# A third place in PSUM for the products of w_up, reordered joints between chunks, and a reordered end in a one-core trunk layer

## The chip, the cores and the metric

One kernel computes one layer of a diffusion backbone on one core of one Trainium2 chip. The metric is the device time in microseconds of one execution; lower is better. The engines named below are TensorE (PE in the rows; PEld is its weight load), VectorE (DVE), ScalarE (ACT), GpSimd (POOL) and SyncE (SP, which issues nearly all DMAs). SBUF is the on-chip memory that all engines work on, PSUM the accumulators that TensorE writes.

## What is computed

The layer has a mixer part (attention and a state-space scan, until about 800 us) and a ConvFFN. The change touches the second alone:

```python
h2 = rmsnorm(x, norm_ffn_g) * (1 + sc2) + sh2
u  = dwconv_centred(h2 @ w_up, ffn_conv_w, ffn_conv_b)      # width 3 along the tokens
x  = x + g2 * ((silu(u[..., :D_FF]) * u[..., D_FF:]) @ w_down)
y  = rmsnorm(x, final_norm_g)
```

There are 640 tokens (128 of a prompt and 512 of a sample, with their own modulation), a width of 1024 and D_FF = 2816. Data and results are float32. Tokens lie along the free axis, features along the 128 partitions.

## The kernel before

Each float32 operand of a matmul is split into a rounded part `hi` and a rest `lo` (line 112 computes the rest, line 115 the rounding), and a product is the sum of hi·hi, hi·lo and lo·hi (`mm3`, line 139).

The 2816 features are 22 tiles of 128. A tile i has two products of w_up: (i,0), the gate, and (i,1), the value. Each takes 8 blocks of the width, three matmuls each, on 384 and 256 columns: 48 matmuls. It goes into one of two PSUM buffers called `big` (two banks each, so that 640 columns fit). The buffers go round, so that product n + 2 has to wait until the convolution of product n has read its buffer. The convolution (`conv`, lines 463 to 468) is one pass on ScalarE (scale and bias of the middle tap) and four on VectorE, which add the two neighbour taps for each of the two token groups. The fourth, line 468 on 511 columns, frees the buffer. Behind the value comes the join: silu on ScalarE (L1258) and the product of gate and value on VectorE (L1434). Tile (1,0) is an exception: its product was made before, in an SBUF tile, and its convolution (`early`) reads SBUF alone.

Beside this runs work for later: the weights of the next products are loaded and split (rounding on ScalarE, rest on GpSimd); after every odd tile the two joined tiles are cut into blocks (`blocks`, L1266 to L1281) and split; and after some tiles `ada_next` computes a column of the modulation on VectorE, two passes over 1024 columns each (L260). The table `ADA` says how many such columns follow tile i.

The tiles come in chunks that begin at 0, 8 and 16 (`CHUNKS`). At the end of a chunk, its tiles times w_down are added to x. Here a fast product for 2×2 blocks is used: seven products instead of eight, with sums and differences of blocks of weights (`Pair.add`, L1330) and of the results (L1361 and the lines below). A pair stands for two output tiles; four pairs make a chunk's 1024 outputs. Each of the seven products takes an operand (`put`), which is a rounding on ScalarE and a rest on GpSimd or, where `ON_DVE` says so, on VectorE. A joint is the place where a chunk ends: the two products of the next tile (nxt,0) and (nxt,1) stand there, then the pairs. `LEAD` = 5 operands are made ahead of the first product of a pair.

At the end, the outputs 4 to 7 of the last chunk are made by plain products (`plain`, L1523): first on 384 columns (c0), then on 256 (c1), 16 matmuls each. Behind each stands `residual` (VectorE, L1098) and a square for the final norm (`finished`, ScalarE, L1535). `sumsq` (L166) adds the squares over the partitions with matmuls of one column; `rstd_cols` (L171, L172) takes the root and the reciprocal, `diag` (L177) puts it on a diagonal, a matmul with ones (L1597, L185) spreads it over the partitions, and `scaled_out` (L1583) scales and issues a DMA to `out_y` for each output and column part: 16 in all, on SP.

The order on the compute engines is partly found by a scheduler when the program is built; within `tc.manual_schedule` (the joints with the pairs, and the end) the order is that of the code, and `issue_after` holds an instruction behind another.

## Time and profile before

| | us |
|---|---|
| three runs: median (lowest, highest) | 1265.67 (1265.47, 1268.54) |
| the profiled execution | 1265.61 |
| its span, first to last instruction | 1263.8 |
| TensorE busy | 1197.4 (95 %) |
| VectorE busy | 861.4 (68 %) |
| ScalarE busy | 589.2 (47 %) |
| GpSimd busy | 498.3 (39 %) |

The span runs from the first instruction to the last; what lies between it and the time of the execution is start and end of the program. Busy shares are means over the whole program. In the rows a name such as `big<-pg,whi` says what is written from what; x4 counts instructions drawn together; the square brackets give the idle time of the engine just before and the engine, buffer and line that ended it. A clock of 1.00 in a window is the full 2.4 GHz of TensorE, 0.50 is 1.2 GHz.

### The profile page before, as it was taken

The numbers are of one execution on the slowest core, as the hardware profiler recorded it, in microseconds if no ns is written. First come the engines' busy times: TensorE is split into PE (matmuls) and PEld (weight loads), VectorE is DVE, ScalarE is ACT, GpSimd is POOL, SyncE is SP. The second block draws the span as 40 slices with busy tenths as digits, with TensorE's granted clock in tenths as the row PEclk, the third lists the DMA queues.
The fourth block names the chain that finished last, engine by engine and source line by source line (L and its number), as shares of the span: only waits on it lengthen the run. The fifth ranks groups of instructions, "written<-read, shape, count | busy, mean of one in ns | idle before, by whom it ended". The sixth has DMA issues, their size and how long they took to land. (4 is left out here: it accounts for less than half of the span.)

```text
span 1263.8 us, 21105 instructions
## 1 busy us (share of the span) xinstructions
PE 1197.4 (95%) x8273; PEld 1144.8 (91%) x8273; DVE 861.4 (68%) x1516; ACT 589.2 (47%) x1086; POOL 498.3 (39%) x304
## 2 busy tenths in 40 slices
PE   7798999999999899999979898999999999999996
PEld 5698999989999898888968897999999999999996
DVE  4766656575547566776869898877785456875755
ACT  5455455544647645544762233544333433434432
POOL 3433121221213342554657484543255333454422
PEclk9999999999999899999979899999999999999998
DMA  8333221222128653312465664233246221362222
GB/s 328 126 104 111 71 71 62 78 72 99 38 92 285 215 193 115 99 66 100 139 228 184 210 223 172 83 117 125 68 143 229 79 70 48 109 201 75 86 74 84
DMA packets 59107, 160.31 MB, mean 127 GB/s; under 512 B 6784, under 2 KB 12736, under 8 KB 59008
## 3 DMA queue, kind: packets, MB, share of 16 engines
q1 hardware_dynamic: 56960, 156.33, 36.5%
q10 hardware_dynamic: 2048, 2.63, 0.7%
q8 instruction: 65, 1.06, 0.4%
q14 instruction: 34, 0.28, 0.1%
HBM read 130.82 MB, written 25.59 MB: 124 GB/s over the span
## 5 line engine op out<-in xcount | busy, mean ns | idle before, releaser
L139 PE MATMUL big<-pg,whi 128*128 128x384 f32 (+2 forms) x3264 | 636.1, 314 | 16.1 <-DVE pg L468 7.9
L139 PEld LDWEIGHTS big<-pg,whi 128*128 128x128 f32 x3264 | 497.8, 189 | 31.3 <-issue 12.4
L112 POOL TENSOR_TENSOR wlo<-raw,whi 128x512 fp32r<-128x512 f32 (+3 forms) x161 | 305.8, 1908 | 539.9 <-ACT whi L115 531.1
L139 PE MATMUL big<-pg,wlo 128*128 128x384 f32 (+2 forms) x1632 | 384.0, 311 | 4.6 <-POOL wlo L112 4.6
L139 PEld LDWEIGHTS big<-pg,wlo 128*128 128x128 f32 x1632 | 255.6, 190 | 5.9 <-POOL wlo L112 5.4
L115 ACT CAST whi<-raw 128x512 fp32r<-128x512 f32 (+3 forms) x186 | 138.1, 758 | 154.3 <-issue 74.1
L139 PE MATMUL sm<-pg,whi 128*128 128x320 f32 (+2 forms) x584 | 135.5, 317 | 7.5 <-ACT pg L115 4.1
L139 PEld LDWEIGHTS sm<-pg,whi 128*128 128x128 f32 x584 | 100.4, 191 | 11.0 <-ACT pg L115 4.4
L139 PE MATMUL sm<-pg,wlo 128*128 128x320 f32 (+2 forms) x292 | 91.8, 314 | 0.4 <-POOL wlo L112 0.4
L465 DVE SCALAR_TENSOR_TENSOR st<-big,vec,st 128x127 f32<-128x127 f32 x68 | 37.0, 544 | 67.6 <-ACT st L463 67.6
L112 POOL TENSOR_TENSOR wlo<-sum,whi 128x512 fp32r<-128x512 f32 (+1 forms) x40 | 50.1, 1275 | 61.3 <-ACT whi L115 61.3
L115 ACT CAST pg<-pg 128x640 fp32r<-128x640 f32 (+1 forms) x60 | 40.4, 706 | 69.5 <-DVE pg L1088 35.1
L112 DVE TENSOR_TENSOR pg<-pg,pg 128x640 fp32r<-128x640 f32 (+1 forms) x57 | 52.7, 949 | 11.4 <-ACT pg L115 11.4
L260 DVE SCALAR_TENSOR_TENSOR araw<-araw,crow 128x1024 f32<-128x1024 f32 x32 | 58.4, 1826 | 0.6
L139 PEld LDWEIGHTS sm<-pg,wlo 128*128 128x128 f32 x292 | 55.9, 191 | 0.7 <-POOL wlo L112 0.7
L112 DVE TENSOR_TENSOR ptl<-sm,pth 128x512 fp32r<-128x512 f32 (+1 forms) x48 | 29.6, 620 | 35.0 <-ACT pth L610 35.0
L594 ACT ACTIVATE p<-sm,st 128x320 f32<-128x320 f32 x64 | 33.1, 523 | 37.7 <-DVE st L592 37.7
L591 DVE TENSOR_REDUCE st<-sm 128x1 f32<-128x320 f32 (+1 forms) x72 | 31.5, 462 | 26.6 <-PE sm L587 26.6
L260 DVE SCALAR_TENSOR_TENSOR junk<-araw,crow 128x1024 f32<-128x1024 f32 x32 | 47.4, 1482 | 0.0
L610 ACT CAST pth<-sm 128x512 fp32r<-128x512 f32 (+1 forms) x48 | 25.5, 533 | 43.6 <-PE sm L607 43.5
L465 DVE SCALAR_TENSOR_TENSOR pg<-big,vec,pg 128x127 f32<-128x127 f32 (+1 forms) x42 | 22.8, 543 | 30.5 <-ACT pg L463 30.5
L115 ACT CAST whi<-sum 128x512 fp32r<-128x512 f32 (+1 forms) x40 | 22.6, 596 | 40.5 <-DVE sum L1330 30.1
(323 smaller groups left out, 1947.3 us busy)
## 6 DMA issues: line engine op xcount, KB each, us to landing
raw<-w_up SPq DMA_DIRECT2D x44, 512.0 KB, 3.5
araw<-w_adar SPq DMA_DIRECT2D x32, 512.0 KB, 4.0
araw<-w_ada SPq DMA_DIRECT2D x16, 512.0 KB, 7.3
raw<-w_down SPq DMA_DIRECT2D x16, 512.0 KB, 3.5
raw<-w_xbc SPq DMA_DIRECT2D x12, 512.0 KB, 3.4
scr_xc<-pg SPq DMA_DIRECT2D x16, 320.0 KB, 3.5
pg<-scr_xc SPq DMA_DIRECT2D x16, 320.0 KB, 4.2
raw<-w_gm SPq DMA_DIRECT2D x8, 512.0 KB, 3.3
```

The source lines that it names most:

```text
L112: return eng.tensor_tensor(out, x, f(hi), ALU.subtract)
L115: ACT.copy(hi, src)
L139: PE.matmul(o, w, r[:, s], start=first and i == 0, stop=last and i == 2, skip_group_check=on)
L260: DVE.scalar_tensor_tensor(out, raw, 1.0, crow[r], ALU.mult, ALU.mult, accum_out=mod[:, j, r : r + 1])
L465: DVE.scalar_tensor_tensor(dst[:, lo_ + 1 : hi_], p[:, lo_ : hi_ - 1], vec[:, w : w + 1], dst[:, lo_ + 1 : hi_], ALU.mult, ALU.add)
L591: DVE.reduce_max(st[:, i : i + 1], sv, AX.X)
L594: ACT.activation(p[:, i * w : (i + 1) * w], sv, AF.Exp, bias=st[:, 2:3], scale=SCALE, accum_out=st[:, 4 + i : 5 + i])
L610: return ph, pl, ACT.copy(ph[:, :n], pt[:, :n]), sub(DVE, pl[:, :n], pt[:, :n], ph[:, :n])
```

## The change

Six things are changed.

1. *A third place in PSUM.* The value product (i,1) of an even tile (2, 4, ... 20) goes into two small PSUM buffers of one bank each (384 and 256 columns), which come from the pool the pairs use; all others stay in `big`. Its convolution, `conv_parts`, has two passes on ScalarE (L1265 of the changed kernel) and six on VectorE (L1273), since the columns lie in two buffers. Before, of the products (2,0), (2,1), (3,0), (3,1), (4,0) each waits for the one two places ahead of it; now (3,0) waits for the buffer of (1,1), (3,1) for that of (2,0), (4,0) for that of (3,0), and (5,0) for that of (3,1).
2. *The start.* The early convolution (1,0) is issued behind the last step of (0,1)'s convolution.
3. *ADA* is (0, 0, 2, 1, 2, 1, 2) instead of (0, 1, 1, 1, 1, 2, 2).
4. *The joint.* The loads for the pairs and the sums of the first pair come one product earlier (with tile (nxt−1,0)); its first five operands come later, all behind silu(nxt,0); and the seventh operand of a chunk's first pair has its rest made on GpSimd. The sums of the next pair stand one behind each product instead of two behind the third.
5. *The last pairs:* sums and operands of their first come after the first plain products.
6. *The end.* The squares of c0 are added on VectorE before `sumsq`, which has three matmuls instead of nine and stands behind product 5 instead of product 4; the spreading matmul comes behind product 6 instead of 5; the outputs of c1 go in four DMAs of two tiles each, issued by SP and ScalarE in turn, to a new output array that the host joins to the rest.

```diff
-LEAD, ON_DVE = 5, (4, 6)
+LEAD, ON_DVE = 5, ((4,), (4, 6))
-ADA = (0, 1, 1, 1, 1, 2, 2)
+ADA = (0, 0, 2, 1, 2, 1, 2)
...
         def product(self):
+            if self.j and self.i % 2 == 0 and self.i:
+                outs = [(small()[:, 0 : c.stop - c.start], c) for c in PARTS]
+                for k in range(8):
+                    (hi, lo), s = self.w[k // 4], slice(k % 4 * 128, k % 4 * 128 + 128)
+                    mm3(outs, hi[:, s], lo[:, s], h2[k], k == 0, k == 7)
+                return [o for o, _ in outs]
             ps = big()
...
+    def conv_parts(dst, ps, w, b):
+        for p, c in zip(ps, PARTS):
+            ACT.activation(dst[:, c], p, AF.Identity, bias=vec[:, b : b + 1], scale=vec[:, w + 1 : w + 2])
+        for d, t in ((-1, 0), (1, 2)):
+            for lo_, hi_ in ((0, NP), (NP, T)):
+                for p, c in zip(ps, PARTS):
+                    r0, r1 = max(c.start, lo_ + (d > 0)), min(c.stop, hi_ - (d < 0))
+                    if r0 < r1:
+                        o = dst[:, r0 - d : r1 - d]
+                        ev = DVE.scalar_tensor_tensor(
+                            o, p[:, r0 - c.start : r1 - c.start], vec[:, w + t : w + t + 1], o, ALU.mult, ALU.add
+                        )
+        return ev
...
-            self.w.append(operand(x, self.n * 128, DVE if n in ON_DVE else POOL))
+            self.w.append(operand(x, self.n * 128, DVE if n in ON_DVE[self.m > 0] else POOL))
...
-                for n in ((), (), (1, 2), (3,), (), (4,), ())[s]:
+                for n in ((), (), (1,), (2,), (3,), (4,), ())[s]:
                     nxt.add(n)
...
-        us[i, j] = up_conv(i, j, p)
+        if (i, j) == (1, 0):
+            with tc.issue_after(after_[0].ins):
+                us[i, j] = up_conv(i, j, p)
+        else:
+            us[i, j] = up_conv(i, j, p)
...
+                if (i, j) == (nxt - 1, 0):
+                    made[i, 1] = Up(i, 1)
+                    made[i, 1].fetch()
+                    ahead = [Up(nxt, 0).load(), Up(nxt, 1).load()]
+                    new = [Pair(c, m) for m in range(0, 8, 2)]
+                    new[0].load()
                 if (i, j) == (nxt - 1, 1):
-                    ahead = [Up(nxt, 0), Up(nxt, 1)]
                     for v in ahead:
                         v.fetch()
-                    new = [Pair(c, m) for m in range(0, 8, 2)]
-                    new[0].load()
+                up_tile(u, early if (i, j) == (1, 0) else None)
+                if (i, j) == (nxt - 1, 0):
                     ready(new[0])
-                    for n in range(LEAD - 1):
-                        new[0].put(n)
-                up_tile(u, early if (i, j) == (1, 0) else None)
...
             silu(us[nxt, 0])
-            new[0].put(LEAD - 1)
+            for n in range(LEAD):
+                new[0].put(n)
...
+        for o, x in ((sq4, sq5), (sq6, sq7), (sq4, acc[:, c0]), (sq4, sq6)):
+            DVE.tensor_tensor(o, o, x, ALU.add)
...
             plain(m, ps, c1, ks)
-            if m == 4:
-                ss = sumsq([acc, sq4, sq6], c0)
...
             if m == 5:
+                ss = sumsq([sum0], c0)
+            if m == 6:
                 rp = small()[:, 0:HALF]
                 PE.matmul(rp, ones, dg, start=True, stop=True)
...
             residual(x2[m], ps, 40 + m, x2[m], c1)
             finished(m, c1, c1 if m < 7 else None)
+            if m == 5:
+                dg = ws.tile([128, HALF], F32, tag="dg", name=nm("dg"), bufs=1)
+                diag(dg, rstd_cols(ss, D, 3))
+            if m == 6:
+                scaled_out(rp, range(4))
...
+        for m in range(8):
+            if m == 1:
+                ACT.copy(rps, rp)
+            o, x = outs[m // 4][:, m % 4], x2[m][:, c1]
+            if m in BY_POOL:
+                POOL.tensor_tensor(o, x, rps, ALU.mult)
+            else:
+                DVE.scalar_tensor_tensor(o, x, vec[:, V_GFIN + m : V_GFIN + m + 1], rp, ALU.mult, ALU.mult)
+            if m % 2:
+                q = nc.sync if m % 4 == 1 else nc.scalar
+                q.dma_start(a["out_z"][:, m - 1 : m + 1], outs[m // 4][:, m % 4 - 1 : m % 4 + 1])
```

Three places show how the instructions move. First VectorE at the start of the ConvFFN, before: `big_8473` holds (0,0) and `big_8536` (0,1); `pg_8325` is the product of (1,0) in SBUF, which the early convolution reads.

```order
L465 SCALAR_TENSOR_TENSOR pg_8522<-big_8473,vec,pg_8522 128x127
L468 SCALAR_TENSOR_TENSOR pg_8522<-big_8473,vec,pg_8522 128x127
L465 SCALAR_TENSOR_TENSOR pg_8522<-big_8473,vec,pg_8522 128x511
L465 SCALAR_TENSOR_TENSOR pg_8593<-pg_8325,vec,pg_8593 128x127
L468 SCALAR_TENSOR_TENSOR pg_8522<-big_8473,vec,pg_8522 128x511
L468 SCALAR_TENSOR_TENSOR pg_8593<-pg_8325,vec,pg_8593 128x127
L465 SCALAR_TENSOR_TENSOR pg_8593<-pg_8325,vec,pg_8593 128x511
L465 SCALAR_TENSOR_TENSOR st_8585<-big_8536,vec,st_8585 128x127
L468 SCALAR_TENSOR_TENSOR pg_8593<-pg_8325,vec,pg_8593 128x511
L468 SCALAR_TENSOR_TENSOR st_8585<-big_8536,vec,st_8585 128x127
```

After, the same place:

```order
L465 SCALAR_TENSOR_TENSOR pg_8522<-big_8473,vec,pg_8522 128x127
L468 SCALAR_TENSOR_TENSOR pg_8522<-big_8473,vec,pg_8522 128x127
L465 SCALAR_TENSOR_TENSOR pg_8522<-big_8473,vec,pg_8522 128x511
L468 SCALAR_TENSOR_TENSOR pg_8522<-big_8473,vec,pg_8522 128x511
L465 SCALAR_TENSOR_TENSOR st_8585<-big_8536,vec,st_8585 128x127
L468 SCALAR_TENSOR_TENSOR st_8585<-big_8536,vec,st_8585 128x127
L465 SCALAR_TENSOR_TENSOR st_8585<-big_8536,vec,st_8585 128x511
L468 SCALAR_TENSOR_TENSOR st_8585<-big_8536,vec,st_8585 128x511
L465 SCALAR_TENSOR_TENSOR pg_8593<-pg_8325,vec,pg_8593 128x127
L1468 TENSOR_TENSOR pg_8522<-pg_8522,st_8585 128x640
L468 SCALAR_TENSOR_TENSOR pg_8593<-pg_8325,vec,pg_8593 128x127
L465 SCALAR_TENSOR_TENSOR pg_8593<-pg_8325,vec,pg_8593 128x511
```

The four steps on (0,0) now stand together, the four on (0,1) follow, and the early convolution's are mixed with the join of tile 0 and its first block difference.

Second, ScalarE at the first joint, before: from the pass over (8,0) (`big1499`) to the copy of the first pair's first result. `whi1501` is the fifth operand; the four ahead of it stand further up, around (7,1).

```order
L463 ACTIVATE pg1500_9662<-big1499_9613,vec_69 128x640
L115 CAST pg1495_9602<-pg1490_9590 128x640
L115 CAST hf1497_9607<-pg1468_9479 128x320
L1258 ACTIVATE pg1500_9662<-pg1500_9662 128x640
L115 CAST whi1501_9669<-raw1478_9509 128x512
L463 ACTIVATE st1508_9730<-big1507_9681,vec_69 128x640
L115 CAST whi1501_9669<-sum1483_9519 128x512
L1358 COPY o31512_9754<-big1509_9739 128x320
```

After; `big1498` is (8,0), `sm1510` and `sm1511` are (8,1):

```order
L463 ACTIVATE pg1499_9662<-big1498_9613,vec_69 128x640
L115 CAST hf1496_9607<-pg1478_9507 128x320
L1288 ACTIVATE pg1499_9662<-pg1499_9662 128x640
L115 CAST whi1500_9669<-raw1475_9454 128x512
L115 CAST whi1500_9669<-sum1480_9515 128x512
L115 CAST whi1502_9675<-sum1481_9517 128x512
L115 CAST whi1502_9675<-sum1479_9513 128x512
L115 CAST whi1504_9681<-raw1475_9454 128x512
L1265 ACTIVATE st1512_9743<-sm1510_9693,vec_69 128x384
L1265 ACTIVATE st1512_9743<-sm1511_9694,vec_69 128x256
L115 CAST whi1504_9681<-sum1482_9519 128x512
L1388 COPY o31516_9770<-big1513_9755 128x320
```

The first five operands of the pair (`whi1500`, `whi1502` and half of `whi1504`) now stand between the silu of (8,0) and the passes over (8,1), where one stood before.

Third, VectorE at the end, before: from the sums of squares to the first scaled output. `sm_13109` and `sm_13110` are the plain products 4 and 5 of c1.

```order
L1577 TENSOR_TENSOR pg_13082<-pg_13082,pg_13089 128x384
L1578 TENSOR_TENSOR pg_13096<-pg_13096,pg_13103 128x384
L172 RECIPROCAL rst_13141<-rst_13141 128x3
L177 TENSOR_SCALAR dg_13144<-cons,rst_13141 128x128 x3
L1098 SCALAR_TENSOR_TENSOR pg_12849<-sm_13109,mod,pg_12849 128x256
L1098 SCALAR_TENSOR_TENSOR pg_12851<-sm_13110,mod,pg_12851 128x256
L1583 SCALAR_TENSOR_TENSOR pg_12841<-pg_12841,vec,sm_13170 128x384
```

After; `sm_13151` and `sm_13152` are products 4 and 5, `sm_13153` is product 6:

```order
L1613 TENSOR_TENSOR pg_13122<-pg_13122,pg_13129 128x384
L1613 TENSOR_TENSOR pg_13136<-pg_13136,pg_13143 128x384
L1613 TENSOR_TENSOR pg_13122<-pg_13122,pg_12748 128x384
L1613 TENSOR_TENSOR pg_13122<-pg_13122,pg_13136 128x384
L1099 SCALAR_TENSOR_TENSOR pg_12889<-sm_13151,mod,pg_12889 128x256
L1099 SCALAR_TENSOR_TENSOR pg_12891<-sm_13152,mod,pg_12891 128x256
L172 RECIPROCAL rst_13204<-rst_13204 128x3
L177 TENSOR_SCALAR dg_13203<-cons,rst_13204 128x128 x3
L1099 SCALAR_TENSOR_TENSOR pg_12893<-sm_13153,mod,pg_12893 128x256
L1620 SCALAR_TENSOR_TENSOR pg_12881<-pg_12881,vec,sm_13228 128x384
```

The reciprocal and the diagonal moved behind the residuals of products 4 and 5, two additions came in, and the first scaled output stands behind product 6's residual.

## Rows read from the trace of the kernel before

**Rows 1.** waits of TensorE from 800 us on; total us, times, longest us

```profile
PE big L139 <- DVE pg L468: 7.9, 4, 3.6
...
PE sm L139 <- DVE o L1361: 1.9, 3, 0.9
```

**Rows 2.** timeline of TensorE; start, us, engine, line, operation, [idle before and releaser]

```profile
806.06 0.82 PE L139 MATMUL big<-pg,whi 128*128 128x384 f32 x4 [1.63 <-DVE pg L468]
...
887.38 0.82 PE L139 MATMUL big<-pg,whi 128*128 128x384 f32 x4 [3.64 <-DVE pg L468]
...
923.47 0.56 PE L139 MATMUL sm<-pg,whi 128*128 128x320 f32 x2 [0.88 <-DVE o L1361]
...
1053.87 0.83 PE L139 MATMUL big<-pg,whi 128*128 128x384 f32 x4 [1.67 <-DVE pg L468]
```

**Rows 3.** windows: length, busy us of PE, PEld, DVE, ACT, POOL; clock, DMA, GB/s

```profile
888.00:893.00 5.00, 5.00 (x26) 5.00 (x25) 4.89 (x9) 0.57 (x2) 1.59 (x1) 0.66 0.34 94
...
1243.00:1248.00 5.00, 5.00 (x29) 4.79 (x28) 1.64 (x6) 0.68 (x2) 0.73 (x1) 0.66 0.01 3
```

**Rows 4.** timeline of VectorE, first tiles of the ConvFFN

```profile
802.93 0.35 DVE L468 SCALAR_TENSOR_TENSOR pg<-big,vec,pg 128x127 f32<-128x127 f32 x1
...
803.86 1.40 DVE L465 SCALAR_TENSOR_TENSOR pg<-pg,vec,pg 128x127 f32<-128x127 f32 x1
...
805.18 0.74 DVE L468 SCALAR_TENSOR_TENSOR pg<-big,vec,pg 128x511 f32<-128x511 f32 x1
...
806.46 1.77 DVE L465 SCALAR_TENSOR_TENSOR pg<-pg,vec,pg 128x511 f32<-128x511 f32 x1
...
831.22 0.82 DVE L1434 TENSOR_TENSOR pg<-pg,st 128x640 f32<-128x640 f32 x1
```

**Rows 5.** timeline of VectorE, from the join of tile 6

```profile
891.55 0.83 DVE L1434 TENSOR_TENSOR pg<-pg,st 128x640 f32<-128x640 f32 x1
...
892.29 1.22 DVE L260 SCALAR_TENSOR_TENSOR junk<-araw,crow 128x1024 f32<-128x1024 f32 x1
...
899.88 0.74 DVE L468 SCALAR_TENSOR_TENSOR pg<-big,vec,pg 128x511 f32<-128x511 f32 x1
```

**Rows 6.** timeline of VectorE, splits at the first joint

```profile
916.19 0.69 DVE L112 TENSOR_TENSOR wlo<-raw,whi 128x512 fp32r<-128x512 f32 x1 [1.37 <-ACT whi L115]
...
921.23 1.78 DVE L112 TENSOR_TENSOR wlo<-raw,whi 128x512 fp32r<-128x512 f32 x1
```

**Rows 7.** timeline of TensorE, the end

```profile
1240.79 0.68 PE L166 MATMUL sm<-cons,pg 128*128 128x1 f32 x4
...
1242.08 1.72 PE L166 MATMUL sm<-cons,pg 128*128 128x1 f32 x14 [0.61 <-DVE pg L1578]
...
1250.19 1.60 PE L1523 MATMUL sm<-pg,pg 128*128 128x256 f32 x12
...
1252.23 0.28 PE L1523 MATMUL sm<-pg,wlo 128*128 128x256 f32 x1
...
1255.54 0.67 PE L185 MATMUL sm<-dg,cons 128*128 128x256 f32 x2 [1.16 <-DVE dg L177]
```

**Rows 8.** timeline of ScalarE, the end

```profile
1241.14 1.28 ACT L171 ACT_TABLE_LOAD   x1
```

**Rows 9.** timeline of VectorE, the end

```profile
1256.65 2.44 DVE L1583 SCALAR_TENSOR_TENSOR pg<-pg,vec,sm 128x256 f32<-128x256 f32 x6 [1.26 <-ACT pg L1608]
```

**Rows 10.** timeline of SyncE's DMA queue, the end

```profile
1260.81 0.40 SPq L1613 DMA_DIRECT2D out_y<-pg  x1
```

**Rows 11.** DMA from 1245 to 1264 us: rate by slice; issues, KB, us to landing

```profile
GB/s 0 0 0 0 0 0 0 0 0 16 352 366 366 142 0 246 362 369 265 49 359 378 42 0 0 0 0 11 272 270 274 274 272 272 267 276 22 0 0 17
...
out_y<-pg SPq DMA_DIRECT2D x8, 128.0 KB, 1.8
```

**Rows 12.** DMA issues of the whole program

```profile
scr_xc<-pg SPq DMA_DIRECT2D x16, 320.0 KB, 3.5
...
out_ssd<-k SPq DMA_DIRECT2D x2, 256.0 KB, 2.0
```

More of the change, by code (lines that the diff above doesn't have):

```diff
@@ L1233, in load @@
             nc.sync.dma_start(self.raw, a["w_up"][2 * self.i + self.j])
+            return self
         def put(self, n):
@@ L1239, in fetch @@
             if not self.w:
-                self.load()
+                if not self.raw:
+                    self.load()
                 self.put(0)
@@ L1250, in product @@
             return mid(ps)
+    def conv_parts(dst, ps, w, b):
[7 more added lines that the diff above has]
+                        o = dst[:, r0 - d : r1 - d]
+                        ev = DVE.scalar_tensor_tensor(
+                            o, p[:, r0 - c.start : r1 - c.start], vec[:, w + t : w + t + 1], o, ALU.mult, ALU.add
+                        )
+        return ev
+    after_ = []
     def up_conv(i, j, p):
         u = stage() if j else page()
-        conv(u, p, V_FW + 3 * (2 * i + j), V_FB + 2 * i + j)
+        ev = (conv_parts if isinstance(p, list) else conv)(u, p, V_FW + 3 * (2 * i + j), V_FB + 2 * i + j)
+        if (i, j) == (0, 1):
+            after_.append(ev)
         return u
@@ L1491, in trunk_kernel @@
                 new[0].load()
-                ready(new[0])
-                for n in range(LEAD):
-                    new[0].put(n)
     def cut(i, c):
@@ L1554, in trunk_kernel @@
         wlast = []
+        ready(new[0])
+        for n in range(LEAD):
+            new[0].put(n)
         new[0].load_x()
@@ L1589, in trunk_kernel @@
             plain(m, ps, c1, ks)
-            if m == 4:
-                ss = sumsq([acc, sq4, sq6], c0)
-                st = rstd_cols(ss, D, 3)
-                dg = ws.tile([128, HALF], F32, tag="dg", name=nm("dg"), bufs=1)
-                diag(dg, st)
             if m == 5:
+                ss = sumsq([sum0], c0)
+            if m == 6:
                 rp = small()[:, 0:HALF]
                 PE.matmul(rp, ones, dg, start=True, stop=True)
-            if m > 5:
-                scaled_out(rp, c0, range(3 * m - 18, 3 * m - 15))
             residual(x2[m], ps, 40 + m, x2[m], c1)
             finished(m, c1, c1 if m < 7 else None)
+            if m == 5:
[3 more added lines that the diff above has]
+                scaled_out(rp, range(4))
         ss = sumsq([acc, sqs[7]], c1)
-        scaled_out(rp, c0, range(6, 8))
+        scaled_out(rp, range(4, 7))
         for m in BY_POOL:
             ACT.activation(x2[m][:, c1], x2[m][:, c1], AF.Copy, scale=vec[:, V_GFIN + m : V_GFIN + m + 1])
-        rp = rstd_rows(ss, D, c1)
-        rps = page()[:, 0:w1]
-        ACT.copy(rps, rp)
-        for m in BY_POOL:
-            POOL.tensor_tensor(x2[m][:, c1], x2[m][:, c1], rps, ALU.mult)
-        scaled_out(rp, c1, [m for m in range(8) if m not in BY_POOL])
-        for m in BY_POOL:
-            nc.sync.dma_start(a["out_y"][m][:, c1], x2[m][:, c1])
+        dg = ws.tile([128, HALF], F32, tag="dg", name=nm("dg"), bufs=1)[:, 0:w1]
+        diag(dg, rstd_cols(ss, D, w1 // 128))
+        scaled_out(rp, range(7, 8))
+        rp = small()[:, 0:w1]
+        PE.matmul(rp, ones, dg, start=True, stop=True)
+        rps = page()[:, 0:w1]
+        outs = [rawtile().rearrange("p (m c) -> p m c", c=w1) for _ in range(2)]
+        for m in range(8):
[9 more added lines that the diff above has]
+                q.dma_start(a["out_z"][:, m - 1 : m + 1], outs[m // 4][:, m % 4 - 1 : m % 4 + 1])
 def _consts():
@@ L1719 @@
 _OUTS = {
-    "out_y": (8, 128, T),
+    "out_y": (8, 128, HALF),
+    "out_z": (128, 8, T - HALF),
     "out_ckv": (2, 128, NP),
```

18 lines of the change are left out of this document (9 added, 9 removed).

## The prediction

> **What bounds the kernel now.** I read the waits of TensorE first, then its timeline at each wait, then what the releasing engine did just before. From 800 us on, where the diff first touches an instruction, TensorE has few stalls, and two releasers hold most of them: the last convolution step (VectorE, L468) frees a `big` buffer too late four times, and L1361 frees a pair's PSUM buffer late three times [rows 1]. So the stage is bound by TensorE and each late release adds to the time directly; VectorE decides when the release comes. The time of a product of w_up follows from two rows: between 806.06 and 887.38 − 3.64 = 883.74 stand 11 products without a gap, 7.06 us each [rows 2]. The longest wait has a second price: after it the granted clock of 888 to 893 us is 0.66, so part of those 5 us ran at 1.2 instead of 2.4 GHz, which loses (1 − 0.66) × 5 = 1.7 us of work; the same 1.7 us is lost after 1243 us [rows 3]. At the end, TensorE's last product is over at 1252.51 (call this X), and 10 us of a serial chain and output transfers follow.
>
> All terms are made against the profiled execution: 1265.61 us, of which 1263.8 are span and 1.8 lie around it. That is the median of the runs (1265.67) within 0.06 us, so I carry gains straight over.
>
> **Start of the ConvFFN.** In before, an SBUF-only convolution step of tile (1,0), 1.40 us (803.86), stands ahead of the L468 that frees the buffer of (0,0); product (1,1) starts at 806.06 after 1.63 us of waiting [rows 2, 4]. After, the order has the four steps of (0,0) together. The release comes at 803.86 + 0.08 + 0.74 = 804.7 instead of 805.18 + 0.74 = 805.9; with 0.05 of spare handover I take **gain 1.3**.
>
> The postponed steps come back later. Steps of (1,0) now stand behind (0,1)'s, which begin behind ScalarE's pass at about 805.6 (by hand) and end at 805.6 + 0.35 + 0.35 + 0.74 + 0.74 = 807.8 (sizes in [rows 4]); with their own four (beside GpSimd's splits the short first took 1.40 and a long one 1.77 in before, so 5 to 6 us), the join of tile 0 and one block difference, they end at about 815.5. The silu of (1,0) stands ahead of (1,1)'s first ACT pass on ScalarE, so conv (1,1) ends at about 820. In before join (2) began at 831.22, 4.0 us behind the end of product (2,1) at 806.06 + 3 × 7.06 = 827.24 [rows 2, 4]; that product now ends 1.3 earlier, and join (2) comes at 830.0 if TensorE alone limits it. If VectorE does, it comes some 13 us behind conv (1,1): join (1), three block differences, four splits and two convolutions, while one ADA step with two passes of 1.22 [rows 5] leaves this stretch; that is an estimate, 833.0. From a join with two ADA steps behind it to the end of the next tile's convolution pass 900.62 − 891.55 = 9.07 us [rows 5]: (3,0)'s buffer comes free at 839.1 to 842.1. The change puts the products (i,1) of even i in the small buffers, and so (4,0) waits for (3,0)'s buffer, which it had not to before; it is due at 840.05 (five products of 7.06 after 804.75). The bounds are 0 and 2.1; I take the later half because the silu is certain to be in the way: **loss 1.5**.
>
> **Steady tiles.** The new rotation of `big` asks that the first convolution of an odd i ends within one product (7.06) of its product's end, for (4,0), (6,0), (8,0) and their like; (7,0) and (15,0) wait for nothing new. The parted convolution has six VectorE steps instead of four: two more starts, at 0.35 − 127 × (0.74 − 0.35)/384 = 0.22 us each, so 0.4 us [rows 4]. An even tile's second product ends at E, its join begins at E + 4.0 as join (2) did, with the parts E + 4.4, the next convolution ends 9.07 later, at E + 13.5, and E + 14.1 (two products) is needed: 0.6 us spare. If these lengthen by more than this, each such tile waits (rival 1). (7,0) no longer waits: 3.64 and the 1.7 of the clock behind it: **gain 5.3** (bounds 3.6 and 5.3). (15,0): **gain 1.67** (bounds 0.8, if half comes back as another wait, and 1.67) [rows 2, 3]. (8,0) is due just when conv (7,0) lands, as sums and two ADA steps lie ahead of it: **loss 0.3**, bounds 0 and 1.2. The fourth wait, 7.9 less the three shown = 0.96 [rows 1], is (20,0)'s; a sum of the last pair still stands ahead of the L468 that frees its buffer, so I leave it: 0, bounds 0 and a gain of 0.96.
>
> **The two joints.** Product 3 waited 0.88 us at 923.47 (and as much at the other joint) for L1361, which stood behind the split L112 of 1.78 us on VectorE [rows 2, 6]. That split goes to GpSimd, and L1361's successor stands right behind the join: I expect 0.3 left. Against this, five splits of the pair's first weights now come after silu(nxt,0) instead of before; the first products' weights are ready near the end of product (nxt,1), so 0.1 lost. **Gain 0.5 at each joint, 1.0 in all**; bounds: all 0.88 gained, and a loss of 1.8 at each, if the first product waits for one whole split beside VectorE. The third place's 0.18, the rest of the 1.9 in [rows 1], I take as gained: **0.2**.
>
> On VectorE the same split takes 0.69 us at 916.19 and 1.78 us at 921.23 [rows 6]. The Trainium skill ("SBUF — State Buffer", section "SBUF: two separate sides") says that VectorE and GpSimd share a port pair which is locked exclusively, the loser standing still. It speaks against this part of the change: more splits on GpSimd next to VectorE's joins would hand the 1.1 us difference between the two rows to the join. By it the joint would gain nothing; by the removed 1.78 alone it gains 0.6.
>
> **The end.** Before, 18 narrow sum-of-squares matmuls stand between products 4 and 5, four from 1240.79 and fourteen from 1242.08 behind a wait of 0.61, and product 5 runs in the stretch of clock 0.66 [rows 3, 7]. After, product 5 follows product 4 directly: 1240.9 + 2.15 = 1243.05 (2.15 is 1252.51 − 1250.19 = 2.32 at full clock, less the 0.17 by which neighbours overlap). Then sums of one tile, a third as many: 0.7; product 6 ends at 1245.9. The row sum's matmul must wait for residual and square behind product 5 (estimated 1.05, so 1244.1), the table load of 1.28 [rows 8], which now stands behind these squares, then root, reciprocal and diagonal (estimated 1.5 with handovers): 1246.9. So a new wait of about 0.9; then about 0.35 for that matmul, half of the 0.67 of its like at 1255.54, since the next product runs into it, and product 7: X' = 1246.9 + 0.35 + 2.15 = 1249.4, **gain 3.1** (bounds: 1.4 if the new wait costs the clock 1.7 again; 4.0 without the wait).
>
> From X to the end of the row sum's second matmul nothing changes, 1255.54 + 0.67 − 1252.51 = 3.7 [rows 7]. VectorE then does its six products of 2.44 us without waiting 0.37 for ScalarE's copy [rows 9]; all outputs are computed at X' + 6.2. Before, the eight issues on SP ran until 1260.81 [rows 10], 8.3 us after X, and the last transfer took 1.8 us from its issue [rows 11]. After there are four transfers of 256 KB by two queues, the last at X' + 6.2. The nearest row for 256 KB to HBM is 2.0 us, the next is 3.5 us for 320 KB [rows 12]; I take 2.0. Last landing at X' + 8.2 instead of X + 10.05: **gain 1.65** (bounds 0.2 and 1.8).
>
> The eight transfers of 128 KB moved at 267 to 276 GB/s [rows 11], so the end may be bound by bytes: 1 MB at 270 GB/s is 3.9 us; begun at X' + 4.6 with about 1 us of latency it ends at X' + 9.5. The Trainium skill ("DMA: Bandwidth & Descriptors", section "Issuing engines are not separate DMA queues") says transfers of all issuing engines share the same 16 engines and a second issuer only saves its sequencer's time. By that rule with this rate the end gains 0.55, by the issue row 1.65.
>
> **Sum.** 1.3 − 1.5 + 5.3 + 1.67 − 0.3 + 1.0 + 0.2 + 3.1 + 1.65 = 12.4 us: 1265.6 − 12.4 = **1253.2 us**.
>
> **Rivals.**
> 1. *Slower: the waits move to the odd tiles.* (4,0), (6,0) and (8,0) now need a buffer that the convolution of the odd tile before frees, with an even tile's join and two ADA steps ahead of it on VectorE. If these 9.07 us grow by g, each waits g − 0.6 and pays 1.7 for the clock as (7,0) did, 3 × (g + 1.1); that eats the remaining gains of 12.4 + 1.5 + 0.3 = 14.2 from g = 3.6 on, 12.7 us in place of 9.07. With g = 6, two sums and a few splits at the slow 1.78, it is 21.3: 1265.6 − 14.2 + 21.3 = 1272.7. For it: sums, splits and ADA steps all stand there. Against: one lengthening beside GpSimd is 1.1 us [rows 6], and it takes four of them in each tile. 5 %.
> 2. *Part of the gain is given back.* (4,0) waits 2.1 and pays 1.7 for the clock, (8,0) 1.2, the joints gain nothing, the new wait at the end costs 1.7: 1253.2 + (2.1 − 1.5) + 1.7 + (1.2 − 0.3) + 1.0 + 1.7 = 1259.1. For it: in both places where TensorE's work thinned out, the clock fell [rows 3]. Against: waits of 1.63 and 1.67 show no lost clock. 24 %.
> 3. *The end is bound by bytes:* 1.1 less gain, 1254.3. 15 %.
> 4. *Better:* (4,0) doesn't wait and (20,0) loses its wait: 1253.2 − 1.5 − 0.96 = 1250.7. 12 %.
> The forecast itself (within 1.5 us) has 44 %.
>
> **How the numbers follow.** A change under 0.3 % (3.8 us) can't be told from none here: faster means below 1261.9, slower above 1269.4. Forecast, rivals 3 and 4 and nearly all of rival 2 are faster: 0.89. The outer part of rival 2, where several of its costs come out above the bounds named, and half of rival 1 (g of 3 to 5) give 0.08 for the same, the rest of rival 1 0.03 for slower. The range reaches from rival 4 less the small bounds (all of the joints' 0.88, no wait at the end) to rival 2: 1248.5 to 1260.
>
> **What would show it.** In the profile of the changed kernel: no wait at (7,0) and (15,0) and no clock below 1.0 behind them (if it stays, the third place did nothing); a wait of 1 to 2 us at (4,0) released by VectorE's L468; none above 1 us at (6,0), (8,0); product 3 of the joints waiting under 0.4 us; TensorE's last product over near 1241.7 us of the new span (1249.4 less the 7.7 gained before the end); the last landing 8.2 us behind it. The prediction is wrong if a wait over 3 us stands at any even tile, or if the first product of a pair waits for GpSimd's split by more than 1 us.

## The result: 0.8 % faster, less than forecast

The changed kernel took 1259.52 us (median of 7 runs), the kernel before 1268.54 (7 runs); the ratio is 0.9922, 95 % interval 0.9904 to 0.9941. Further rounds of both gave 0.9939, 0.9917 to 0.9962. So the change gains some 8 to 10 us where 12.4 were forecast, and its time lies near the upper end of the forecast range. The kernel before took 2.9 us more in these runs than the 1265.67 that the forecast starts from; the ratio applied to 1265.67 gives 1255.8. One of the changed kernel's seven runs, the one profiled first, took 2304.72 us: in it a matmul of 256 columns into `big` took 0.44 us in the mean instead of 0.28, though the granted clock on record is 1.00; that stays unexplained, and the profile read here is that of another execution, e1.

**A common mark.** The instructions ahead of the ConvFFN are those of before, but the time at which they are done differs by up to 7.7 us between the profiled executions, more than most edits here are worth. So I count from a mark that all kernels share: the end of the last sum-of-squares matmuls ahead of the first w_up product. These are its rows in TensorE's timeline, of before and of after:

```profile
787.48 0.83 PE L166 MATMUL sm<-cons,pg 128*128 128x1 f32 x6 [0.47 <-ACT pg L1120]
```

```profile
793.17 0.83 PE L166 MATMUL sm<-cons,pg 128*128 128x1 f32 x6 [0.48 <-ACT pg L1121]
```

The marks are 788.31 and 794.00. Where the instructions are the same, times from the mark agree within 0.2 us: (8,0) begins 112.25 to 112.42 us behind it in e1, e3, e4 and e7. In microseconds from the mark, one profiled execution of each kernel (e2 to e12 are told of below):

| | first plain product | last plain product ends (X) | end of span | against after |
|---|---|---|---|---|
| before | 415.80 | 464.21 | 475.52 | +9.58 |
| after (e1) | 409.64 | 455.13 | 465.94 | 0 |
| e2, no third place | 412.35 | 457.83 | 468.68 | +2.74 |
| e3, old sums at the end | 409.44 | 457.49 | 468.41 | +2.47 |
| e4, eight transfers | 409.51 | 454.99 | 466.32 | +0.38 |
| e5, a column later | 410.62 | 456.10 | 466.43 | +0.49 |
| e6, early convolution in its old place | 406.92 | 452.40 | 463.25 | −2.69 |
| e7, seventh operand on VectorE | 413.27 | 458.75 | 469.60 | +3.66 |
| e8, third place alone, in before | 413.69 | 460.59 | 471.91 | +5.97 |
| e9, early convolution behind (0,0) | 405.75 | 451.23 | 461.56 | −4.38 |
| e10, old ADA | 408.82 | 454.31 | 464.63 | −1.31 |
| e11, sums behind the join | 408.49 | 453.98 | 464.31 | −1.63 |
| e12, e9 with the row sums spread twice | 405.79 | 451.28 | 461.18 | −4.76 |

The change gains 9.58 us behind the mark: 6.16 up to the first plain product, 2.92 in the plain products, 0.50 at the end.

**The profile after.** TensorE's waits from 800 us on (total, times, longest):

```profile
PE big L139 <- DVE pg L468: 3.0, 2, 2.3
PE sm L1648 <- DVE dg L177: 1.2, 1, 1.2
PE sm L166 <- ACT pg L1569: 0.9, 1, 0.9
PE sm L1632 <- DVE dg L177: 0.7, 1, 0.7
PE big L139 <- ACT whi L115: 0.5, 1, 0.5
```

Four late buffers became two, and L1361's three waits [rows 1] are gone. TensorE's timeline says which are left:

```profile
810.60 0.82 PE L139 MATMUL big<-pg,whi 128*128 128x384 f32 x4 [0.46 <-ACT whi L115]
...
848.29 0.82 PE L139 MATMUL big<-pg,whi 128*128 128x384 f32 x4 [2.25 <-DVE pg L468]
...
1175.42 0.82 PE L139 MATMUL big<-pg,whi 128*128 128x384 f32 x4 [0.77 <-DVE pg L468]
```

The first answers to 806.06 of [rows 2]: product (1,1) now waits 0.46 us, for its weights. The second is new: (4,0), five products later. The third is (20,0)'s. At (7,0), (8,0), (15,0) and in both joints no matmul waits. The windows (columns as in [rows 3]) show that the clock fell behind the new wait, and again in the last microseconds:

```profile
848.00:853.00 5.00, 4.71 (x21) 4.74 (x22) 2.73 (x6) 2.54 (x4) 2.57 (x2) 0.66 0.35 137
...
1252.00:1255.00 3.00, 1.15 (x2) 0.46 (x2) 1.75 (x5) 0.37 (x1) 0.70 (x2) 0.53 0.40 148
```

The wait at (4,0) thus costs 2.25 + (1 − 0.66) × 5 = 3.95 us. VectorE's timeline, from the early convolution on, shows why it comes:

```profile
813.44 1.32 DVE L465 SCALAR_TENSOR_TENSOR pg<-pg,vec,pg 128x127 f32<-128x127 f32 x1
814.68 1.92 DVE L1468 TENSOR_TENSOR pg<-pg,st 128x640 f32<-128x640 f32 x1
816.51 1.37 DVE L468 SCALAR_TENSOR_TENSOR pg<-pg,vec,pg 128x127 f32<-128x127 f32 x1
817.81 1.78 DVE L465 SCALAR_TENSOR_TENSOR pg<-pg,vec,pg 128x511 f32<-128x511 f32 x1
...
838.07 0.83 DVE L1468 TENSOR_TENSOR pg<-pg,st 128x640 f32<-128x640 f32 x1
...
840.07 2.19 DVE L260 SCALAR_TENSOR_TENSOR araw<-araw,crow 128x1024 f32<-128x1024 f32 x1
...
842.20 2.30 DVE L260 SCALAR_TENSOR_TENSOR junk<-araw,crow 128x1024 f32<-128x1024 f32 x1
...
847.41 0.73 DVE L468 SCALAR_TENSOR_TENSOR pg<-big,vec,pg 128x511 f32<-128x511 f32 x1
```

The postponed short steps take 1.32 and 1.37 us, a long one 1.78, and the join of tile 0 between them 1.92; GpSimd splits weights beside them all the while, and again from 839.48 on (GpSimd's timeline):

```profile
809.56 9.48 POOL L112 TENSOR_TENSOR wlo<-raw,whi 128x512 fp32r<-128x512 f32 x7 [0.81 <-ACT whi L115]
...
839.48 3.93 POOL L112 TENSOR_TENSOR wlo<-raw,whi 128x512 fp32r<-128x512 f32 x2 [1.52 <-ACT whi L115]
```

Join (2) begins at 838.07, where TensorE alone would have allowed about 836.2 (product (2,1) ends at 810.60 + 3 × 7.06 = 831.8; the forecast had the join 4.4 behind it). Then two of the four passes of the modulation columns, 1.22 us in [rows 5], take 2.19 and 2.30 beside GpSimd's two splits. From the join to the end of (3,0)'s convolution pass 848.14 − 838.07 = 10.07 us instead of 9.07. By the Trainium skill ("SBUF — State Buffer", section "SBUF: two separate sides") VectorE and GpSimd lock a shared port pair against each other; that the same pass has two lengths agrees with it.

### The profile page after: what moved, and what is told of

Read it like the earlier page. It is cut to its first block, busy times and chain, and to the rows that moved or that the text cites. A ratio compares the mean times of both kernels' runs of the same rounds, so it can differ in the third digit from the quotient of the medians.

```text
span 2302.8 us, 21101 instructions
## 1 busy us (share of the span) xinstructions
PE 2288.3 (99%) x8261; PEld 2062.9 (90%) x8261; DVE 812.8 (35%) x1535; ACT 599.5 (26%) x1096; POOL 472.4 (21%) x307
## 4 chain that ended last, share of the span: by engine, by line
PE 99%; DVE 0%; DMA 0%; ACT 0%; SPq 0%; issue 0%; DVEq 0%
PE big L139 56%; PE sm L139 26%; PE sm L617 3%; PE sm L1557 2%; PE sm L608 2%; PE sm L588 2%; PE big L363 1%; PE sm L986 1%; PE sm L1026 1%; PE sm L219 1%; PE sm L908 1%; PE sm L1034 1%; PE sm L363 1%; PE sm L166 1%; PE sm L957 0%; PE sm L875 0%
## 5 line engine op out<-in xcount | busy, mean ns | idle before, releaser
L139 PE MATMUL big<-pg,whi 128*128 128x384 f32 (+2 forms) x2944 | 1032.3, 501 | 0.0
L139 PEld LDWEIGHTS big<-pg,whi 128*128 128x128 f32 x2944 | 798.9, 306 | 77.8 <-issue 42.3
L139 PE MATMUL big<-pg,wlo 128*128 128x384 f32 (+2 forms) x1472 | 591.9, 498 | 0.0
L112 POOL TENSOR_TENSOR wlo<-raw,whi 128x512 fp32r<-128x512 f32 (+3 forms) x164 | 281.9, 1726 | 1401.8 <-ACT whi L115 1393.9
L139 PEld LDWEIGHTS big<-pg,wlo 128*128 128x128 f32 x1472 | 406.7, 306 | 29.6 <-issue 11.9
L139 PE MATMUL sm<-pg,whi 128*128 128x320 f32 (+2 forms) x904 | 344.5, 500 | 0.0
L139 PEld LDWEIGHTS sm<-pg,whi 128*128 128x128 f32 x904 | 260.2, 310 | 16.8 <-issue 7.0
L139 PE MATMUL sm<-pg,wlo 128*128 128x384 f32 (+2 forms) x452 | 210.1, 501 | 0.0
L139 PEld LDWEIGHTS sm<-pg,wlo 128*128 128x128 f32 x452 | 133.2, 308 | 8.2 <-issue 3.6
L465 DVE SCALAR_TENSOR_TENSOR st<-big,vec,st 128x127 f32<-128x127 f32 (+1 forms) x48 | 26.1, 544 | 136.0 <-ACT st L463 136.0
L1273 DVE SCALAR_TENSOR_TENSOR st<-sm,vec,st 128x127 f32<-128x127 f32 (+2 forms) x60 | 22.6, 433 | 91.0 <-ACT st L1265 89.9
```

The lines of the kernel that those rows point to most:

```text
L112: return eng.tensor_tensor(out, x, f(hi), ALU.subtract)
L139: PE.matmul(o, w, r[:, s], start=first and i == 0, stop=last and i == 2, skip_group_check=on)
L465: DVE.scalar_tensor_tensor(dst[:, lo_ + 1 : hi_], p[:, lo_ : hi_ - 1], vec[:, w : w + 1], dst[:, lo_ + 1 : hi_], ALU.mult, ALU.add)
```

## The experiments

Each is one edit. The waits are those of one profiled execution, and "slower" and "faster" go by the table above. The differences include what the clock did in that execution: as it fell or held with the same instructions, up to 1.7 us at (4,0) and 0.5 at the end are chance. By whole runs against the kernel before, the ratios of all twelve lie between 0.9888 and 0.9977, with intervals of some ±0.002 to ±0.0026 each; these alone tell few of them apart.

**e1, the changed kernel again,** without an edit.

> The changed kernel unaltered, for a profile at the clock of the kernel before. By the prediction's terms: 12 us less than before; no wait of TensorE at (7,0) and (15,0); one of about 1.5 us at (4,0), released by the last convolution step of (3,0); 0.3 us at product 3 of the joints; about 0.9 us ahead of the matmul that spreads the row sums of the first 384 columns; last landing 8.2 us behind the last plain product. By the rival that part is given back: 7 to 8 us less than before, waits over 2 us at (4,0) or (8,0) with a granted clock under 1 behind them, and the clock lost once more at the end.

Measured: above. (7,0), (15,0), (8,0) and the wait ahead of the spreading matmul (0.75) came out by the prediction, (4,0) by the rival, the joints better than either.

**e2, no third place.**

```diff
-            if self.j and self.i % 2 == 0 and self.i:
+            if False:
```

> The changed kernel with all products of w_up in the two large buffers again, everything else kept. If the third place carries the gain as the prediction has it (5.3 + 1.67 gained, 1.5 + 0.3 lost): 5.2 us slower than the changed kernel, with a wait of 3 us or more at (7,0), a granted clock under 1 behind it, about 1.7 us at (15,0) and none at (4,0). If instead the moved sums and the new order of the modulation's columns took these waits away: within 1 us of the changed kernel, and no wait over 1 us at (7,0).

Measured: 2.74 us slower, between the two. (7,0) and (15,0) wait again, and (3,0) and (6,0) (the first two lines) wait too:

```profile
832.15 0.82 PE L139 MATMUL big<-pg,whi 128*128 128x384 f32 x4 [1.45 <-DVE pg L468]
...
875.53 0.83 PE L139 MATMUL big<-pg,whi 128*128 128x384 f32 x4 [0.78 <-DVE pg L468]
...
891.74 0.83 PE L139 MATMUL big<-pg,whi 128*128 128x384 f32 x4 [1.89 <-DVE pg L468]
...
1055.64 0.82 PE L139 MATMUL big<-pg,whi 128*128 128x384 f32 x4 [1.74 <-DVE pg L468]
```

At (15,0) the third place is worth all of its 1.7 us. At (7,0) the wait is 1.89 us instead of 3.64 [rows 2], and the clock holds. That does not mean that the reordered sums and columns free the buffer earlier: (7,0) begins 99.42 us behind the mark in e2 and 99.07 in before. TensorE only comes later to it, having waited at (3,0) and (6,0). So without the third place the other orders spread the wait over three products, which saves the clock; with it, in e1, (7,0) begins at 98.15 although (4,0) has lost 3.95 us, and the pairs behind (8,1) begin at 126.57 instead of 127.66.

**e8, the third place alone,** in the kernel before: `product` and `conv_parts` as in the change, nothing else.

> The kernel before with the third place alone (products (i,1) of even i in two small buffers, convolution in parts). If the third place takes away the waits at (7,0) and (15,0) by itself: both gone, the half clock behind (7,0) too, 6 to 7 us less than before, the waits at (1,1), product 3 and the end unchanged. If it needs the other orders beside it: a wait of over 1.5 us at (4,0), (6,0) or (8,0) takes their place and less than 4 us are gained.

Measured: ratio 0.9977 (0.9956 to 0.9997); 3.61 us less than before by the table, 1.5 of them in the plain products, where the clock did not fall this time. (7,0) and (15,0) wait for nothing, but (8,0), 13 products behind (1,1), does, and its clock falls:

```profile
907.51 1.20 PE L139 MATMUL big<-pg,whi 128*128 128x384 f32 x4 [3.73 <-DVE pg L468]
```

On VectorE sums and modulation columns stand mixed between the join of tile 6 and the convolution of (7,0). Two of them are slow beside GpSimd's splits. One of these splits (last line) is for an operand of the pair, which the change makes later:

```profile
898.38 1.76 DVE L1353 TENSOR_TENSOR sum<-raw,raw 128x512 f32<-128x512 f32 x1
900.06 2.31 DVE L260 SCALAR_TENSOR_TENSOR araw<-araw,crow 128x1024 f32<-128x1024 f32 x1
...
899.55 1.73 POOL L112 TENSOR_TENSOR wlo<-sum,whi 128x512 fp32r<-128x512 f32 x1
```

Alone, the third place hands the wait at (7,0) on by two products.

**e11, the sums behind the join.**

```diff
-                    ready(new[0])
+                    with tc.issue_after(joins[nxt - 2].ins):
+                        ready(new[0])
```

> The changed kernel with the first pair's four sums held behind the join of tile nxt-2, where the kernel before had three of them. If the third place needs the moved sums (each takes 0.7 us or more between the join of tile 6 and the convolution of (7,0)): a wait of 2.0 to 4 us at (8,0) with half the clock behind it, 3.7 to 5.7 us slower than the changed kernel; none at (16,0), since no modulation columns stand there. If the columns of the modulation alone decide: no wait over 0.5 at (8,0).

Measured: no wait at (8,0), so my theory that the third place needs the moved sums fell; (6,0) waits 0.77. The run was even 1.63 us faster than e1 (by whole runs 0.9898 of before, 0.9873 to 0.9923), for another reason: (4,0) waits the same 2.25 us, but the clock held behind it, and at the end it fell later. TensorE's timeline, then the window behind (4,0):

```profile
841.79 0.82 PE L139 MATMUL big<-pg,whi 128*128 128x384 f32 x4 [2.25 <-DVE pg L468]
...
870.96 0.82 PE L139 MATMUL big<-pg,whi 128*128 128x384 f32 x4 [0.77 <-DVE pg L468]
```

```profile
841.00:846.00 5.00, 4.21 (x29) 4.24 (x30) 2.75 (x5) 2.54 (x4) 2.58 (x2) 1.00 0.45 177
```

**e10, the old ADA:** (0, 1, 1, 1, 1, 2, 2).

> The changed kernel with the old table ADA (0,1,1,1,1,2,2). If VectorE's queue from the early convolution to (3,0) is what counts, it makes no difference behind which of the tiles 1 and 2 a column stands: the wait at (4,0) stays between 1 and 3 us, and two columns behind tile 5 add a wait of 1 us or more at (8,0). If the column behind tile 2 alone makes (4,0) late: no wait there, 4 us faster.

Measured: 1.31 us faster, as the first expectation had the waits: one at (4,0), one at (8,0), both without loss of the clock:

```profile
842.26 0.83 PE L139 MATMUL big<-pg,whi 128*128 128x384 f32 x4 [1.48 <-DVE pg L468]
...
900.38 0.82 PE L139 MATMUL big<-pg,whi 128*128 128x384 f32 x4 [1.56 <-DVE pg L468]
```

So (8,0) waits for nothing with the sums behind the join alone (e11), 1.56 us with the old columns alone (e10) and 3.73 in e8, which has both. But the sums are not what e8 has on top: from the join of tile 6 to the end of (7,0)'s convolution pass 8.70 us in e11, 8.69 in e10 and 10.88 in e8, and the 2.2 more are the two slow steps shown there (0.68 and 1.22 us in e10). With the old columns the join itself begins later, 6.96 us behind the end of its product in e10 and e8, against 4.72 in e11 and 5.09 in e1. That the later operands of the change keep GpSimd away from these steps is argued, not shown: no run moves them alone. The new ADA takes 1.56 away at (8,0) and adds 0.77 at (4,0), and in e1 that cost the clock too.

**e5, a column later:** ADA (0, 0, 1, 2, 2, 1, 2).

> The changed kernel with one column of the modulation moved from behind tile 2 to behind tile 3: ADA (0,0,1,2,2,1,2). If the wait of 2.25 us at (4,0) comes from VectorE's queue (join of tile 2, two columns, then the convolution of (3,0)): the column's two passes of 1.2 to 2.3 us go, the wait with them (under 0.3 left), and the 3.4 us at half clock behind it too: 3.7 to 4.0 us faster than the changed kernel from the first w_up product to the end. If the wait comes from the third place itself or from ScalarE: still over 1.5 us, no change beyond 1 us. If it only moves: a wait of over 1 us at (5,1) or (6,0).

Measured: the wait at (4,0) goes, and comes back larger at (6,0), nine products behind (1,1), with loss of the clock:

```profile
873.87 0.82 PE L139 MATMUL big<-pg,whi 128*128 128x384 f32 x4 [3.40 <-DVE pg L468]
```

Two columns behind tile 3 and two behind tile 4 stand ahead of (5,0)'s convolution. The third expectation held; this is rival 1's mechanism, at one tile.

**e6, the early convolution in its old place.**

```diff
-        if (i, j) == (1, 0):
-            with tc.issue_after(after_[0].ins):
-                us[i, j] = up_conv(i, j, p)
-        else:
-            us[i, j] = up_conv(i, j, p)
+        us[i, j] = up_conv(i, j, p)
```

> The changed kernel with the early convolution of (1,0) back where the scheduler puts it, mixed into the convolution of (0,0). If its later place is what makes (1,1), join (1) and join (2) late: the wait at (1,1) is back at about 1.6 us (1.2 lost), the wait at (4,0) falls under 0.5 and keeps its clock (3.5 or more gained), in all 2 to 2.8 us faster. If the two modulation columns behind tile 2 alone make (4,0) late: the wait there stays at 1.0 to 2.3 us, and the kernel is up to 1.2 us slower.

Measured: 2.69 us faster. (1,1) waits 1.63 us again, (4,0) not at all, although two columns still stand behind tile 2. The postponed early convolution is what makes (4,0) late; it costs more than it gains. What moves is join (2): it begins 42.52 us behind the mark, in e1 44.07. From there to the release of (3,0)'s buffer pass 9.83 us here and 10.07 in e1, as GpSimd's splits lengthen VectorE's steps in both, here two steps of the columns on 128x2 (1.25 and 0.98 us instead of 0.22).

**e9, the early convolution in between,** behind the last step of (0,0):

```diff
-        if (i, j) == (0, 1):
+        if (i, j) == (0, 0):
             after_.append(ev)
```

> The changed kernel with the early convolution issued behind the last step of (0,0)'s convolution instead of (0,1)'s. If each of the two effects follows from the place alone: the wait at (1,1) stays at about 0.5 us or less, (4,0) waits under 0.5 and keeps its clock; 3.5 to 4 us less than the changed kernel, and 1.0 to 1.2 less than with the early convolution at its old place. If the slow steps beside GpSimd make the chain late wherever they stand: a wait of over 1 us at (4,0) again.

Measured: 4.38 us faster than e1, 1.69 faster than e6, of which 3.90 and 1.17 lie ahead of X; the rest is the clock, which fell later at the end. Ratio to before 0.9891 (0.9866 to 0.9916). Both gains at once, and join (2) begins 41.34 us behind the mark; of the waits ahead of the plain products two are left, at (20,0) and for the weights of (1,1):

```profile
PE big L139 <- DVE pg L468: 0.9, 1, 0.9
...
PE big L139 <- ACT whi L115: 0.4, 1, 0.4
```

**e7, the seventh operand on VectorE:** `ON_DVE` is (4, 6) for every pair.

> The changed kernel with the rest of the seventh operand of a chunk's first pair made on VectorE again. If that split behind the join was what product 3 waited for: 0.9 us of wait is back at both joints, 1.8 us slower than the changed kernel, in which these waits are gone. If the reordered operands removed the wait, because GpSimd no longer works beside this split: the split takes about 0.7 us, no wait over 0.3, no change.

Measured: 3.66 us slower. Product 3 waits 1.82 and 1.41 us, and the split has its slow length (TensorE's timeline, then VectorE's):

```profile
927.73 0.53 PE L139 MATMUL sm<-pg,whi 128*128 128x320 f32 x2 [1.82 <-DVE o L1391]
```

```profile
925.42 1.76 DVE L112 TENSOR_TENSOR wlo<-raw,whi 128x512 fp32r<-128x512 f32 x1
```

That is more than the 0.88 of before, as the join in front of the split now ends 0.4 us ahead of product 3's due time, and in before 1.3. The move to GpSimd is worth 3.2 us of the change as it stands; without it the joints would have lost 1.5. In e1 the join there took 0.98 us instead of 0.83, so of the 1.1 us that the prediction's counter-argument hands to the join 0.15 came; the two sums behind it took 1.38 and 1.62 us instead of 0.68 and 0.69, where TensorE does not wait for them.

**e3, the old sums at the end:** the nine sums behind product 4, their spreading behind product 5.

> The changed kernel with the nine sum-of-squares matmuls of the first 384 columns behind plain product 4 again, their spreading matmul behind product 5 and the scaled outputs where they were. By the prediction: 3.1 us slower, from a wait of 0.6 us ahead of the sums, half the clock behind them (1.7 us), and 18 narrow records in place of 6. If the new wait ahead of the spreading matmul costs the clock as well, only 1.4 us slower; if the order at the end doesn't matter because transfers end last, under 0.5.

Measured: 2.47 us slower, 2.56 in the plain products (48.05 instead of 45.49), nearest to the first expectation. The wait, 0.62, and the clock of 0.66 from 1243 to 1248 us were back.

**e4, eight transfers at the end.**

```diff
-            if m % 2:
-                q = nc.sync if m % 4 == 1 else nc.scalar
-                q.dma_start(a["out_z"][:, m - 1 : m + 1], outs[m // 4][:, m % 4 - 1 : m % 4 + 1])
+            if m not in BY_POOL:
+                nc.sync.dma_start(a["out_z"][:, m], o)
+        for m in BY_POOL:
+            nc.sync.dma_start(a["out_z"][:, m], outs[m // 4][:, m % 4])
```

> The changed kernel with the last 256 columns sent as eight transfers of 128 KB, all issued by SyncE (the two tiles that GpSimd scales last), in place of four of 256 KB issued by two engines. If the issues limit the end: about 1.3 us slower (eight issues 0.48 us apart behind the first output). If the bytes limit it: less than 0.4 us either way, with the rate in the last microseconds near 270 GB/s in both.

Measured: by the table only 0.38 us slower, but in e4 the spreading matmul ahead of the transfers was shorter. From the first scaled output of the last columns (1248.37 in e4, 1253.34 in e1) to the end of the span pass 7.42 us in e4 and 6.61 in e1: the transfers cost 0.8, between the two expectations. The rate by slice, near the end of each row, was 260 to 273 GB/s in e4 and 371 to 388 in e1; the line above it is the busy share of the DMA engines in tenths. First e4, then e1:

```profile
DMA  1000000000000002999929990555207777775000
GB/s 33 0 0 0 0 0 0 0 0 0 0 16 0 0 0 111 360 369 363 363 101 360 360 360 9 206 188 182 80 35 264 268 260 273 266 264 205 0 0 16
```

```profile
DMA  0000000000000001999938995082002999995000
GB/s 0 0 0 0 0 0 0 0 0 0 0 17 0 0 0 65 362 362 362 372 133 307 356 382 197 0 323 91 0 0 95 388 371 375 384 384 211 0 0 0
...
out_z<-raw ACTq DMA_DIRECT2D x2, 256.0 KB, 2.4
```

In e4 the pace is that of the issues. SyncE issued the last six of the eight 0.49 us apart (1250.52 to 1252.97), as the last seven in before (1257.88 to 1260.81). Each landed 1.9 to 2.0 us behind its issue, and 128 KB in 0.49 us are 267 GB/s. Slices of 0.11 us (e4, 1250.5 to 1255 us) show the rate rise to 391 GB/s and fall to 100 between them:

```profile
GB/s 0 0 0 46 273 373 319 146 191 391 319 237 137 328 355 301 100 255 337 364 173 191 337 337 264 119 291 364 310 128 228 346 346 237 18 0 0 0 0 0
```

**e12, the row sums spread twice,** on top of e9:

```diff
-        rp = small()[:, 0:w1]
-        PE.matmul(rp, ones, dg, start=True, stop=True)
+        rp, rq = small()[:, 0:w1], small()[:, 0:w1]
+        for r_ in (rp, rq):
+            PE.matmul(r_, ones, dg, start=True, stop=True)
...
-                ACT.copy(rps, rp)
+                ACT.copy(rps, rq)
```

> As the variant with the early convolution behind (0,0), and at the end the spreading matmul twice, into two PSUM buffers, one read by VectorE and one by ScalarE's copy. If the second scaled output of the last 256 columns waits 0.44 us for that copy because both read one buffer: no such wait, the last scaled output on VectorE 0.4 us earlier behind the last plain product, the end up to 0.4 earlier. If the transfers limit the end: no change beyond 0.15.

Measured: from X to the end 9.90 us instead of e9's 10.33, 0.43 less. By whole runs 1254.06 us, 0.9888 of before (0.9862 to 0.9914): the fastest of all, though runs alone can't tell e9 from it. VectorE's timeline in e1, and in e12:

```profile
1253.34 0.48 DVE L1659 SCALAR_TENSOR_TENSOR raw<-pg,vec,sm 128x256 f32<-128x256 f32 x1 [0.81 <-PE sm L1648]
1254.26 2.05 DVE L1659 SCALAR_TENSOR_TENSOR raw<-pg,vec,sm 128x256 f32<-128x256 f32 x5 [0.44 <-ACT pg L1654]
```

```profile
1241.63 2.44 DVE L1660 SCALAR_TENSOR_TENSOR raw<-pg,vec,sm 128x256 f32<-128x256 f32 x6 [0.33 <-PE sm L1649]
```

In both the first scaled output begins as soon as the matmul allows, in e9 and e12 3.73 us behind X. In e1 the second waits 0.44 us until ScalarE has copied the same buffer; in e12 the six run through. The Trainium skill has a rule for it ("PSUM — Partial Sum Buffer", section "PSUM bank collisions raise a hardware error"): two engines may not access one PSUM bank at once, even if both only read, so the scheduler of the compiler puts a dependency between them. The trace agrees: in e1 the copy and the scaled outputs run one behind the other.

## Why the prediction was right, and where it was not

| term | forecast | measured, e1 against before |
|---|---|---|
| (1,1) | +1.3 | 1.63 − 0.46 = +1.17 |
| (4,0) | −1.5 | −2.25 − 1.7 = −3.95 |
| (7,0) | +5.3 | +5.34 |
| (8,0) | −0.3 | 0 |
| (15,0) | +1.67 | +1.67 |
| joints | +1.0 | +1.76 |
| the third 0.18, and (20,0) | +0.2 | +0.18 + 0.17 |
| plain products | +3.1 | +2.92 |
| end | +1.65 | +0.50 |
| sum | +12.4 | +9.76; by the table +9.58 |

- **What bounds it: right.** Up to X nearly the whole difference lies in TensorE's waits and the clock behind them. None of the signs named for a wrong prediction came: no wait over 3 us at an even tile, and no first product of a pair that waits over 1 us for a split.
- **(4,0): mis-sized.** Place and releaser were forecast, with bounds of 0 to 2.1 us. It was 2.25, and the 1.7 for the clock that only rival 2 had was lost too. Two steps were too small. The 9.07 us from join to convolution, taken from tile 6, were 10.07 here, as GpSimd's splits fell on the columns' passes; with 9.07 the wait would have been 1.25. And the forecast put nothing down for the clock, since 1.63 and 1.67 us had not cost it. Join (2) came 44.07 us behind the mark, within the forecast's 41.7 to 44.7 but 2.7 later than in e9; e6 and e9 show the place of the early convolution to be the cause.
- **(7,0) and (15,0): right in size, half right in cause.** For (15,0) it is the third place (e2). At (7,0) neither part does it alone: without the third place (7,0) begins no earlier than before, with its wait spread over (3,0), (6,0) and (7,0) (e2), and the third place alone hands the wait on to (8,0) (e8). With both, (7,0) waits for nothing even where TensorE comes 4 us earlier to it (e9).
- **Joints: mis-sized, on the good side.** The split taken off VectorE is worth 3.2 us here (e7), and no matmul of the joints waits for the operands behind silu(nxt,0).
- **Plain products: right.** The new wait was 0.75 instead of 0.9, without loss of the clock; e3 gives 2.56 of the 2.92 back.
- **End: mis-sized.** The forecast's own steps, X' + 8.2 instead of X + 10.05, give 1.85, not 1.65. The last transfer was issued 7.2 us behind X instead of 6.2: 0.44 are the step "without waiting 0.37 for ScalarE's copy" (e12), 0.48 the spreading matmul, which took 1.15 us instead of 0.67 [rows 7] as the clock fell while it ran; in e9 to e11, with the same instructions, it fell behind it. It landed 2.5 us behind its issue instead of 2.0, with the DMA engines busy 96 % and more at some 380 GB/s. So bytes do bound the last stretch, as rival 3 had it, but not at its 270 GB/s, which was the pace of SyncE's issues (e4).

Rival 2 described (4,0), and none of its other terms came; rival 1 appeared at one tile in e5 and in e8, where it was forecast for three at once. Not tried by themselves: the sums of the next pair one behind each product, the operands ahead of silu(nxt,0), and e9 without the third place.

## What to carry to other kernels

A longer rotation of buffers removes a wait only if the engine that frees them has the time; otherwise the wait comes back some products later (e5, e8), so look first at what stands between two releases on that engine. A shorter wait is no gain by itself: compare when the product begins, from a common mark (e2). An instruction pushed back off one critical chain can stand at the head of the next one: try the places between the old and the new (e9 beats both). Before counting on two engines that read one PSUM buffer side by side, see whether one waits for the other.
